# Two SwiGLU layers around a merged attention and retention: the odd 256 columns first, as plain products

## Chip, cores and metric

One core of one Trainium2 chip. The metric is device time of one execution in microseconds (us); the median of several runs is compared.

## What is computed

The input x has 512 rows of 1024 float32 values. One decoder layer is applied:

```
x = x + 1/2 * SwiGLU_1(RMSNorm(x))
h = RMSNorm(x); p = h @ w_in
a = NSA(p) @ w_branch_nsa ; r = Retention(p) @ w_branch_ret
x = x + (sigmoid(g_a) * a + sigmoid(g_r) * r) @ w_out
x = x + 1/2 * SwiGLU_2(RMSNorm(x))
out = RMSNorm(x) * final_norm

SwiGLU(x) = (silu(x @ w_gate) * (x @ w_up)) @ w_down     (1024 -> 2816 -> 1024)
RMSNorm(x) = x * rsqrt(mean(x*x) + 1e-6) * gain
```

NSA is an attention of 16 heads with three branches. Retention has 8 heads (key size 64, value size 128); its causal scores are multiplied by a decay, and each head's output is centred, divided by its own root mean square over 128 values and multiplied by a gain.

## The kernel before

Three stages follow each other: `ffn1`, `mix` (attention, retention and their output projections) and `ffn2`. All products are made from float32 values split into a rounded high part and a rest (`split`, L42): ScalarE (ACT) copies the high half at L45, VectorE (DVE) subtracts for the low half at L51, and TensorE (PE) adds three products in the fast 32-bit type f32r, high by high, high by low and low by high. Sums over partitions are products with a matrix of ones, in plain fp32.

**Gate and up** (`gate_up`, L369) go through the 2816 columns in blocks, five of 512 and one of 256 at the end. Each block is one `fast_block` (L261): x's transpose and the two weights are cut into halves of 256 rows and of 512 inner values, and seven Strassen products take the place of eight (order 1, 7, 2, 6, 5, 4, 3). A product has two units of 12 matmuls of 512 columns, 24 in all (in the last block one unit of 24 with 256 columns). The left operands A1 to A7 are made once per FFN from the four quarters of x (`scaled` L232 applies the gain on ACT, `combine` L236 forms s1, s2, s3 and s4, here named so, on DVE and splits all); the right operands are combined from loads on DVE (`put`, L278) and split for each product into the rings whi (3 buffers) and wlo (4). The gated results of a block are transposed by PE (`turn`, L380) behind product 1 of the next block.

**FFN 1's start** (L445 on): x is loaded in eight pieces, PE transposes each 128-column group over all 512 rows, ACT scales it, and `combine` runs after each half. The three norm gains come by three loads of single 4-byte elements (L1247).

**FFN 2's start**: the first half of the operands is made while w_out still runs, the second after its last product. `natural` transposes x back (L1175), 32 transposes in the first block.

**Down** (`down`, L406) needs eight PSUM accumulators, from a pool of its own that follows the pool of gate and up.

**Retention** (`ret_batch` L850, `ret_stage` L874, `ret_head` L896, `ret_norm` L933) runs with a background of gate and branch projections. `weave` (L145) issues the main generator under a raised priority of 400 and pulls background by credit. A head's scores are products at L909 and L910 into banks of a pool of three (name ra), which the transposes of q and k use too; its norm is one fp32 product over ones at L937, then a root on ACT, a reciprocal on DVE and a product on GpSimd.

The order on each engine is not that of the code: a scheduler places every instruction by its own model of the time and by the priorities.

Of the kernel before, what the change touches and what calls it, by code (L numbers as in the profile page):

```python
# [23 lines left out]
BLOCKS = (512,) * 5 + (256,)  # L24
FB = (6, 3, 3, 4)
# [11 lines left out]
class Layer:  # L37
# [158 lines left out]
    def rstd(self, pool, nat=False):  # L196
# [4 lines left out]
        nc.tensor.matmul(ps, self.ones, self.ss, start=True, stop=True)  # L201
# [10 lines left out]
    def lay(self, gu, tags):  # L212

        rings = dict(kept=FB[0], passing=FB[1], whi=FB[2], wlo=FB[3])
        for tag in tags:
            for _ in range(rings.get(tag, 2)):
                gu.tile([128, 4, 256], F32, name="lay", tag=tag, bufs=rings.get(tag, 2))

# [17 lines left out]
    def combine(self, q, act, A, X):  # L236
        nc = self.nc
        sub, add = ALU.subtract, ALU.add

        def hl(p, src):  # L240
            n = 4 // len(A[p][0])
            for i, (h, l) in enumerate(zip(*A[p])):
                self.split(h, l, src[:, i * n:i * n + n])

        if q == 0:
            hl(1, X[0][0])
            s3 = self.act_tile(act, "s3", [128, 4, 256])
            nc.vector.tensor_tensor(s3, X[0][0], X[0][1], op=sub)
            hl(7, s3)
            return  # L250
        hl(2, X[1][0])
        s1, s2 = [self.act_tile(act, n, [128, 4, 256]) for n in ("s1", "s2")]
        nc.vector.tensor_tensor(s1, X[0][1], X[1][1], op=add)
        nc.vector.tensor_tensor(s2, s1, X[0][0], op=sub)
        hl(6, s2)
        hl(5, s1)
        hl(4, X[1][1])
        nc.vector.tensor_tensor(X[1][0], X[1][0], s2, op=sub)
        hl(3, X[1][0])

    def fast_block(self, n, b, gu, psum, A, rn, between):  # L261

        nc = self.nc
        W = BLOCKS[b]
        f0 = sum(BLOCKS[:b])
        kk = 1024 // W
        nu = 4 // kk
# [33 lines left out]

        def product(ps, p, on=False):
            h, l = [[z[:, k] for z in pieces for k in range(z.shape[1])] for pieces in A[p]]
            for i in range(nu):
                src = need(p, i)
                hi = gu.tile([128, kk, W], F32R, name="whi", bufs=FB[2])
                lo = gu.tile([128, kk, W], F32R, name="wlo", bufs=FB[3])
                self.split(hi, lo, src)
# [11 lines left out]
            between.get(p, lambda: None)()  # L320
# [48 lines left out]
    def gate_up(self, n, gu, act, psum, A, rn, between):  # L369
# [4 lines left out]
        def turn(nat, W):  # L374
            for j in range(W // 128):
# [7 lines left out]
        for b, W in enumerate(BLOCKS):  # L383
            nat = self.fast_block(n, b, gu, psum, A, rn, between)
            between = {1: lambda nat=nat, W=W: turn(nat, W)}
        between[1]()
        return out

    def down_weights(self, n, dn, j, tail):

        W = []
        for k in (2 * j, 2 * j + 1):
            W.append([])
            for c in range(2):
                raw = (self.ring if j else dn).tile([128, 1, 512], F32, name="raw", bufs=4)
# [10 lines left out]
    def down(self, n, dn, psum, act, loads, tail, nat):  # L406


        acc = [psum.tile([128, S], F32, name="mm") for _ in range(8)]
# [13 lines left out]
        for j in range(NF // 2):  # L423
# [21 lines left out]
    def ffn1(self):  # L445
# [3 lines left out]
        with tp(name="gu", bufs=1, reuse_waits="tile") as gu, tp(name="ps1", bufs=2, space=PSUM, reuse_waits="tile") as psum:  # L449
            self.lay(gu, ("kept", "whi", "A3", "wlo", "A5", "A4", "A6", "A2", "A7", "A1", "passing"))  # L450
            xin = [gu.tile([128, D], F32, name="xin", tag=f"A{p}", bufs=2) for p in (5, 5, 3, 3)]
            for c in range(2):
                for t in range(NT):
                    cs = slice(c * 512, c * 512 + 512)
                    nc.sync.dma_start(out=xin[t][:, cs], in_=a["x"][0, t * 128:t * 128 + 128, cs])
            sums = self.small.tile([128, NT, 2], F32, name="sums", bufs=1)
            xT = [self.act_tile(act, "xT") for _ in range(4)]
            A, X = self.operands(gu, range(1, 8)), self.quarters(act)
            for k in range(ND):
                ps = psum.tile([128, S], F32, name="mm", tag=("pb", "pc", "tt")[k % 3], bufs=2)  # L460
                for t in range(NT):
                    nc.tensor.transpose(ps[:, t * 128:t * 128 + 128], xin[t][:, k * 128:k * 128 + 128], self.ident)
                self.scaled("ffn1_norm", k, ps, X)
                x = xT[k // 2][:, k % 2]
                nc.vector.tensor_copy(x, ps)
                nc.scalar.dma_start(out=self.xdram[k], in_=x)
                if k % 4 == 3:
                    self.combine(k // 4, act, A, X)
            rn = []

            def norm():
                for t in range(NT):
# [3 lines left out]
                ms = self.small.tile([128, NT], F32, name="ms4", bufs=1)  # L476
                nc.vector.tensor_tensor(ms, sums[:, :, 0], sums[:, :, 1], op=ALU.add)
                sd = self.small.tile([128, NT], F32, name="sd", bufs=2)
                nc.scalar.activation(sd, ms, AF.Sqrt, bias=self.eps, scale=1.0 / D)
                rn.append(self.small.tile([128, NT], F32, name="rn", bufs=2))  # L480
                nc.vector.reciprocal(rn[0], sd)

            norm()
            out = self.gate_up(1, gu, act, psum, A, lambda: rn[0], {})
        self.xt = tc.alloc_tile_pool(name="xt", bufs=1, reuse_waits="tile")
        self.xl_pool = tc.alloc_tile_pool(name="xl", bufs=1, reuse_waits="tile")
        self.xh, self.xl = [[z.tile([128, S], F32R, name=n, bufs=8) for _ in range(8)] for z, n in ((self.xt, "xh"), (self.xl_pool, "xl"))]
        self.mc = tc.alloc_tile_pool(name="mc", bufs=1, reuse_waits="tile")
        with tp(name="dn", bufs=1, reuse_waits="tile") as dn, tp(name="ps1d", bufs=8, space=PSUM, reuse_waits="tile") as psum:
# [12 lines left out]
            self.down(1, dn, psum, out, loads, tail, False)  # L502
            self.first = self.primed(self.dense_N(None, a["w_in"][0], C_KC, 512, ND, self.xh, self.xl))
        act.release()
# [369 lines left out]
    def ret_stage(self, h, T):  # L874
# [15 lines left out]
        if self.ret_tail:  # L890
            yield from self.ret_norm()
        if self.ret_next:
            yield from self.ret_head(*self.ret_next)
        self.ret_next = h, dec, T, vh, vl

    def ret_head(self, h, dec, T, vh, vl):  # L896
# [5 lines left out]
        for js in ((0,), (1, 3), (2,)):  # L902
# [16 lines left out]
            self.split(sh[:, 0:off], sl[:, 0:off], sd[:, 0:off], "act", "pool" if 1 in js else "dve")  # L919
            yield 1.8  # L920
            if pv:
# [8 lines left out]
        self.ret_tail = sq, r  # L930
        yield 1.0

    def ret_norm(self):  # L933
        nc = self.nc
        sq, r = self.ret_tail
        ps = self.psR.tile([128, S], F32, name="ra")
        nc.tensor.matmul(ps, self.ones, sq, start=True, stop=True)  # L937
# [42 lines left out]
    def mix(self):  # L980
# [11 lines left out]
        with tp(name="m", bufs=1, reuse_waits="tile") as self.m:  # L992
# [54 lines left out]
            with tp(name="psM4", bufs=4, space=PSUM, reuse_waits="tile") as pool, \  # L1047
# [22 lines left out]
                def retention():  # L1070
                    for b in range(4):
                        yield from self.ret_batch(b)
                    yield from self.ret_norm()
# [30 lines left out]
                self.xT = []  # L1104
                for k in range(ND):
# [7 lines left out]
                for c in range(2):  # L1113
# [11 lines left out]
        self.xl_pool.release()  # L1125
# [28 lines left out]
    def ffn2(self):  # L1154
# [3 lines left out]
        with tp(name="gu2", bufs=1, reuse_waits="tile") as gu, tp(name="ps2", bufs=2, space=PSUM, reuse_waits="tile") as psum:  # L1158
            self.lay(gu, ("kept", "passing", "A5", "A3", "A4", "A6", "whi", "A2", "wlo"))
            gu.tile([128, 4, 256], F32R, name="lay", tag="wlo", bufs=FB[3])  # L1160
            A, X = {**self.A2, **self.operands(gu, (5, 3, 4, 6, 2))}, self.X2
            for k in range(4, ND):
                self.scaled("ffn2_norm", k, self.xT[k], X)
            self.combine(1, act, A, X)
# [15 lines left out]
            out = self.gate_up(2, gu, act, psum, A, lambda: rn[0], {7: norm, 6: natural})  # L1180
        self.xt.release()
        with tp(name="dn2", bufs=1, reuse_waits="tile") as dn, tp(name="ps2d", bufs=8, space=PSUM, reuse_waits="tile") as psum:
            for n in ("ah", "al"):
                for _ in range(1 + TAIL // 2):
                    dn.tile([128, 2, 512], F32R, name=n, bufs=1 + TAIL // 2)
            for n in ("raw", "o"):
                for _ in range(4):
                    dn.tile([128, S], F32, name=n, bufs=4)
            fin = dn.tile([128, D], F32, name="fin", bufs=1)
            x = [dn.tile([128, D], F32, name="x", bufs=4) for _ in range(NT)]  # L1190
# [126 lines left out]
```

## Time and profile before

| | us |
|---|---|
| median of 3 runs (lowest, highest) | 1382.78 (1382.48, 1384.65) |
| the profiled execution | 1383.53 |
| its span | 1381.8 |
| PE busy | 1341.4 |
| DVE busy | 947.5 |
| ACT busy | 745.1 |
| PE idle, waiting for high halves (L45) in gate and up | 15.5 |

The profile describes one execution. Its page has the busy time of each engine over the span; the other views group waits, follow the chain of waits that ended last, cut the span into stretches, or list instructions in order of time. Start times are in us from the span's start. The duration of a matmul in a timeline overlaps with the next one's, so in a stream the distance of two starts is its price.

### The profile page before, as it was taken

What the parts mean: (1) busy time and instruction counts of PE and PEld (TensorE: products, weight loads), DVE (VectorE), ACT (ScalarE), POOL (GpSimd) and SP (SyncE); (2) the same over time, 40 slices, a digit from 0 to 9 for tenths busy, and PEclk for the clock granted to TensorE, in tenths of its full rate; (3) what the DMA queues carried; (4) which work ended last, traced back from release to release, by engine and by line L of the source; (5) the groups of instructions that cost most, each with busy time, mean ns of one, the idle gap of its engine ahead of it and who ended that gap; (6) DMA issues with size and microseconds to landing.
All of it is one profiled execution on the core that took longest, in us unless ns stands there. A gap on an engine that the chain in (4) does not pass through costs nothing.

```text
span 1381.8 us, 19828 instructions
## 1 busy us (share of the span) xinstructions
PE 1341.4 (97%) x7122; PEld 1143.5 (83%) x7122; DVE 947.5 (69%) x1594; ACT 745.1 (54%) x1348; POOL 318.6 (23%) x379
## 2 busy tenths in 40 slices
PE   6999999999999999999999999999979999999997
PEld 4788889788899889999997888887867888897886
DVE  6977887534545779877778788647667778874342
ACT  7555555434446656856774546444456565554243
POOL 0000000000211077768645335713220000000001
PEclk9999999999999999999999999999989999999999
DMA  8554441624425431112115334435436544424231
GB/s 289 183 167 147 145 137 63 204 92 140 153 73 156 122 89 43 47 47 85 47 49 176 126 101 132 133 132 197 146 114 221 168 142 149 136 92 160 99 122 62
DMA packets 120707, 175.73 MB, mean 127 GB/s; under 512 B 15904, under 2 KB 54432, under 8 KB 120608
## 3 DMA queue, kind: packets, MB, share of 16 engines
q1 hardware_dynamic: 106304, 151.77, 35.5%
q10 hardware_dynamic: 13024, 18.50, 3.7%
q0 software_dynamic: 1280, 4.20, 0.8%
q8 instruction: 56, 0.92, 0.3%
q14 instruction: 43, 0.35, 0.1%
HBM read 157.65 MB, written 16.78 MB: 126 GB/s over the span
## 4 chain that ended last, share of the span: by engine, by line
PE 88%; DVE 5%; DMA 3%; ACT 2%; issue 1%; POOL 1%; ACTq 0%; SPq 0%; DVEq 0%; POOLq 0%
PE mm L317 27%; PE mm L67 16%; PE mm L68 16%; PE mm L69 16%; PE t L777 2%; PE o L793 2%; PE o L792 2%; PE tt L380 1%; DVE wlo L51 1%; PE s L748 1%; PE s L749 1%; DMA ffn_norm<-in_ffn_norm_dram 1%; DMA b<-in_ffn_w_gate_dram 1%; ACT whi L45 1%; DMA b<-in_ffn_w_up_dram 1%
## 5 line engine op out<-in xcount | busy, mean ns | idle before, releaser
L317 PE MATMUL mm<-whi,Ah 128*128 128x512 f32 (+1 forms) x672 | 251.6, 380 | 15.8 <-ACT whi L45 15.5
L317 PE MATMUL mm<-whi,Al 128*128 128x512 f32 (+1 forms) x672 | 249.7, 377 | 0.0
L51 DVE TENSOR_TENSOR wlo<-raw,whi 128x512 fp32r<-128x512 f32 (+1 forms) x184 | 139.8, 770 | 145.8 <-ACT whi L45 143.2
L45 ACT ACTIVATE whi<-raw 128x512 fp32r<-128x512 f32 (+1 forms) x208 | 128.0, 623 | 206.4 <-PE mm L68 106.7
L45 ACT ACTIVATE whi<-b 128x1024 fp32r<-128x1024 f32 x154 | 161.2, 1060 | 119.9 <-PE mm L317 98.1
L51 DVE TENSOR_TENSOR wlo<-b,whi 128x1024 fp32r<-128x1024 f32 x154 | 187.5, 1227 | 46.2 <-ACT whi L45 45.8
L317 PE MATMUL mm<-wlo,Ah 128*128 128x512 f32 (+1 forms) x672 | 176.4, 376 | 2.5 <-DVE wlo L51 2.5
L317 PEld LDWEIGHTS mm<-whi,Ah 128*128 128x128 f32 x672 | 127.9, 191 | 41.0 <-ACT whi L45 18.8
L317 PEld LDWEIGHTS mm<-whi,Al 128*128 128x128 f32 x672 | 128.2, 191 | 21.6
L317 PEld LDWEIGHTS mm<-wlo,Ah 128*128 128x128 f32 x672 | 120.0, 190 | 27.2 <-DVE wlo L51 5.7
L278 DVE TENSOR_TENSOR b<-b,b 128x1024 f32<-128x1024 f32 x88 | 107.2, 1219 | 33.3 <-DMA b<-in_ffn_w_up_dram 33.0
L67 PE MATMUL mm<-whi,xh 128*128 128x256 f32 (+2 forms) x416 | 127.6, 308 | 0.0
L68 PE MATMUL mm<-wlo,xh 128*128 128x256 f32 (+2 forms) x416 | 126.9, 306 | 0.0
L69 PE MATMUL mm<-whi,xl 128*128 128x256 f32 (+2 forms) x416 | 126.6, 305 | 0.0
L754 ACT ACTIVATE P<-P,nm 128x128 f32<-128x128 f32 (+3 forms) x128 | 71.3, 559 | 34.0 <-DVE nm L753 33.3
L51 POOL TENSOR_TENSOR wlo<-raw,whi 128x512 fp32r<-128x512 f32 x56 | 73.7, 1317 | 66.1 <-ACT whi L45 64.7
L760 POOL TENSOR_SCALAR P<-P,rc,sgn 128x128 f32<-128x128 f32 (+3 forms) x128 | 76.9, 612 | 45.7 <-DVE rc L757 22.5
L68 PEld LDWEIGHTS mm<-wlo,xh 128*128 128x128 f32 x416 | 78.9, 190 | 3.4 <-issue 0.2
L67 PEld LDWEIGHTS mm<-whi,xh 128*128 128x128 f32 x416 | 78.7, 190 | 3.4 <-issue 0.2
L69 PEld LDWEIGHTS mm<-whi,xl 128*128 128x128 f32 x416 | 78.8, 190 | 3.1
L1223 POOL TENSOR_TENSOR x<-x,fin 128x512 f32<-128x512 f32 x4 | 5.1, 1286 | 324.2 <-ACT sq L1219 324.2
L67 PE MATMUL mm<-xh,whi 128*128 128x512 f32 x192 | 75.8, 395 | 0.0
(325 smaller groups left out, 3052.5 us busy)
## 6 DMA issues: line engine op xcount, KB each, us to landing
b<-in_ffn_w_up_dram SPq DMA_DIRECT2D x88, 512.0 KB, 4.4
raw<-in_w_in_dram SPq DMA_DIRECT2D x104, 256.0 KB, 2.8
b<-in_ffn_w_gate_dram SPq DMA_DIRECT2D x44, 512.0 KB, 3.8
raw<-in_ffn_w_down_dram SPq DMA_DIRECT2D x88, 256.0 KB, 2.7
rdram<-rsp ACTq DMA_DIRECT2D x16, 256.0 KB, 2.3
raw<-in_w_branch_nsa_dram SPq DMA_DIRECT2D x16, 256.0 KB, 2.7
raw<-in_w_branch_ret_dram SPq DMA_DIRECT2D x16, 256.0 KB, 2.7
raw<-in_w_out_dram SPq DMA_DIRECT2D x16, 256.0 KB, 2.9
```

The lines of the kernel that those rows point to most:

```text
L45: nc.scalar.activation(hi, src, AF.Copy)
L51: eng.tensor_tensor(lo, src, hi.bitcast(F32), op=ALU.subtract)
L67: mm(ps, ah, bh, start=start, stop=False)
L68: mm(ps, ah, bl, start=False, stop=False)
L69: mm(ps, al, bh, start=False, stop=stop)
L278: nc.vector.tensor_tensor(o, x, y, op=op)
L317: nc.tensor.matmul(ps[t][:, 0:W], y[K][:, t * 128:t * 128 + 128], (hi, lo)[w][:, k], start=not on and K == 0 and w == 0 and y is h, stop=l ...
L754: nc.scalar.activation(pb, pb, AF.Exp, scale=-1.0, bias=nm[:, br:br + 1], accum_out=sm[:, br:br + 1])
L760: nc.gpsimd.tensor_scalar(P[:, br, 0:w], P[:, br, 0:w], rc[:, br:br + 1], gate, op0=ALU.mult, op1=ALU.mult)
L777: nc.tensor.transpose(ps[:, n * w + j * 128:n * w + j * 128 + 128], P[:, br, j * 128:j * 128 + 128], self.ident)
L792: nc.tensor.matmul(o[:, q0:q1], v, PT[0][:, br, j, cs], start=half == 0 and br == 0 and j == 0, stop=False)
L793: nc.tensor.matmul(o[:, q0:q1], v, PT[1][:, br, j, cs], start=False, stop=False)
```

## The change

The 256 odd columns come first in each FFN, by 96 plain products of 512 columns (256 of gate beside 256 of up) in place of the seven Strassen products of 256 at the end. Five 512-column Strassen blocks follow, in the product order 1, 2, 7, 6, 5, 4, 3, with both loads of a product issued before its first split. In FFN 1, x is loaded, transposed and scaled by quarters, of 256 rows by 512 inner values, each ahead of the plain products that use it; s3, s1, s2, s4 and their splits are made inside the first Strassen block (`later`). In FFN 2 the weights of the plain block's first half are split while w_out runs. One PSUM pool with four tags holds the banks of gate and up and of down; down's products for its first two inner pieces come before the last transposes. The gains are loaded as rows and transposed by one PE instruction. Sums of squares for `rstd` and for the eight heads are split and made by two f32r products. A head's norm is issued behind the first scores of the next head, and the first head's scores are issued without raised priority. The core of the diff:

```diff
-BLOCKS = (512,) * 5 + (256,)
+W0, NB = 256, 5
...
-            if ahead:
+            if ahead and self.lead:
                 with self.tc.high_priority(offset=ahead):
...
-        nc.tensor.matmul(ps, self.ones, self.ss, start=True, stop=True)
+        sh, sl = [self.tmp.tile([128, S], F32R, name=n, tag="sq", bufs=2) for n in ("ssh", "ssl")]
+        self.split(sh, sl, self.ss)
+        nc.tensor.matmul(ps, self.onesR, sh, start=True, stop=False)
+        nc.tensor.matmul(ps, self.onesR, sl, start=False, stop=True)
...
+    def later(self, act, A, X):
...
+        def s3():
+            self.both(A[7], combined("s3", X[0][0], X[0][1], ALU.subtract))
+        def s2():
+            combined("s1", X[0][1], X[1][1], ALU.add)
+            self.both(A[6], combined("s2", new["s1"], X[0][0], ALU.subtract))
+        def s4():
+            self.nc.vector.tensor_tensor(X[1][0], X[1][0], new["s2"], op=ALU.subtract)
+            self.both(A[3], X[1][0])
+        return {(1, 0): s3, (2, 0): s2, (7, 0): lambda: self.both(A[5], new["s1"]), (6, 0): s4}
...
+    def plain_block(self, n, psum, Q, units, rn, hooks):
...
+        acc = [psum.tile([128, 512], F32, name="mm", tag=tag, bufs=2) for tag in ("pb", "pb", "pc", "pc")]
+        for q in range(2):
+            W = None
+            for u in range(2):
+                hooks.get((q, u), lambda: None)()
+                W = W or units(q)
+                h, l = self.by_k(Q[u][q])
+                for i, (hi, lo) in enumerate(W):
+                    for w in range(2):
+                        for k in range(2):
+                            for y in ((h, l), (h,))[w]:
+                                for t in range(2):
+                                    nc.tensor.matmul(acc[2 * u + t], y[2 * i + k][:, t * 128:t * 128 + 128], (hi, lo)[w][:, k],
+                                                     start=q == i == w == k == 0 and y is h, stop=q == i == w == k == 1)
...
+            srcs = [need(p, i) for i in range(nu)]
...
+                if i == 0:
+                    hook(p, 0)
...
+        Y = banks("p" + ty)
+        product(Y, 2)
+        lower = gated(s1, Y, 0)
         Z = banks("p" + tz)
         product(Z, 7)
         sZ = snap(Z)
-        Y = banks("p" + ty)
-        product(Y, 2)
-        lower = gated(s1, Y, 0)
         product(X, 6, True)
...
+            if j == 0:
+                for i in range(8):
+                    if i == 3:
+                        turn((0, 1))
+                    if i == 6:
+                        turn((2, 3))
+                        acc += [psum.tile([128, S], F32, name="mm", tag="tt", bufs=2) for _ in range(2)]
+                    for k in (0, 1):
+                        mm(i, k, a, W)
+                continue
...
+            out, turn = self.gate_up(1, gu, act, psum, A, Q, units, lambda: rn, {
+                (0, 0): lambda: quarter(0, 0), (0, 1): lambda: quarter(1, 0), (1, 0): lambda: quarter(0, 1), (1, 1): rest},
+                self.later(act, A, X))
...
-        if self.ret_tail:
-            yield from self.ret_norm()
         if self.ret_next:
+            if h == 1:
+                yield 2.0
+                self.lead = False
+                yield 0.0
             yield from self.ret_head(*self.ret_next)
...
+            self.lead = True
             yield 1.8
+            if self.ret_tail and 0 in js:
+                yield from self.ret_norm()
...
-        nc.tensor.matmul(ps, self.ones, sq, start=True, stop=True)
+        nc.tensor.matmul(ps, self.onesR, sh, start=True, stop=False)
+        nc.tensor.matmul(ps, self.onesR, sl, start=False, stop=True)
...
-                        self.combine(0, act, self.A2, self.X2)
+                        self.both(self.A2[1], self.X2[0][0])
+                        self.both(self.A21, self.X2[0][1])
+                        self.w2 = tc.alloc_tile_pool(name="w2", bufs=1, side="right", reuse_waits="tile")
+                        self.early = []
...
-            nc.scalar.dma_start(out=g, in_=a[n][0].rearrange("(k p) -> p k", p=128))
+            nc.scalar.dma_start(out=self.graw[i * ND:i * ND + ND, :], in_=a[n][0].rearrange("(k p) -> k p", p=128))
```

**FFN 1's start on ACT.** The operands of the left side are Ah (high) and their DVE partner Al; xg are scaled quarters, whi weights. Before, after the squares of x:

```order
L45 ACTIVATE Ah_154<-s3_198 128x1024 [waits DVE_49]
L45 ACTIVATE whi_297<-b11_295 128x1024 [waits DMAHW4_49]
L466 DMA xdram_69<-xT_140 128x512 [waits DMAHW0_49,DVE_49]
L45 ACTIVATE Ah_144<-xg_158 128x1024 [waits Activation_49]
L45 ACTIVATE Ah_148<-xg_159 128x1024 [waits Activation_49]
L45 ACTIVATE whi_324<-b12_319 128x1024 [waits DVE_49]
```

and now, in rows 41 to 50 of the engine:

```order
L573 ACTIVATE sd_140<-ms4_391,both_80 128x2 [waits DVE_49]
L45 ACTIVATE Ah_150<-xg_164 128x1024 [waits Activation_49]
L556 ACTIVATE xg_165<-tt_349,gain_84 128x256 [waits PE_49]
L556 ACTIVATE xg_165<-tt_349,gain_84 128x256
L556 ACTIVATE xg_165<-tt_359,gain_84 128x256 [waits PE_49]
L556 ACTIVATE xg_165<-tt_359,gain_84 128x256
L45 ACTIVATE whi_321<-b0_186 128x1024 [waits DMAHW1_49,PE_49]
L45 ACTIVATE Ah_160<-s3_453 128x1024 [waits DVE_49]
L45 ACTIVATE Ah_154<-xg_165 128x1024 [waits Activation_49]
L45 ACTIVATE whi_437<-b11_433 128x1024 [waits PE_49]
```

The last quarter's operand (now Ah_154) stands behind the squares and the scaling of all four quarters, and behind the first Strassen combination (Ah_160, of s3).

**The first head's scores on PE** (rT are the transposed q and k of that head; Oh and whi, xh belong to the background). Before:

```order
L910 MATMUL ra<-rT_8353,rT_8355 128x384
L909 MATMUL ra<-rT_8353,rT_8354 128x128
L910 MATMUL ra<-rT_8353,rT_8355 128x128
L67 MATMUL mm<-whi,xh 128x512
...
L909 MATMUL ra<-rT_8353,rT_8354 128x256 [waits DVE_49,PE_49]
L910 MATMUL ra<-rT_8353,rT_8355 128x256
L67 MATMUL mm<-Oh,whi 128x512 [waits PE_49,Activation_49]
```

and now (L1043 and L1044 are the lines L909 and L910 of before):

```order
L1043 MATMUL ra<-rT_8271,rT_8272 128x128
L1044 MATMUL ra<-rT_8271,rT_8273 128x128
L1044 MATMUL ra<-rT_8271,rT_8273 128x512
L67 MATMUL mm<-whi,xh 128x512
...
L1043 MATMUL ra<-rT_8271,rT_8272 128x256 [waits DVE_49,PE_49]
L1044 MATMUL ra<-rT_8271,rT_8273 128x256
L67 MATMUL mm<-Oh,whi 128x512 [waits PE_49,Activation_49]
```

The earlier score products stand elsewhere among the background's; the third pair, which waits for a bank, stands behind nine background products in both, and ahead of the same one.

**FFN 2's first Strassen block on DVE**, between products 7 and 6 on PE. wlo are low halves of weights (11384 for product 5, unit 0), xg the quarters, Al the low halves of A5 (10955), A6 (10961) and A3 (10957). Before, the sums s1 and s2 stood directly behind the last additions to x, ahead of the first block:

```order
L1117 TENSOR_TENSOR xT_10572<-xT_10572,mm_10777 128x512 [waits DMASW7_49,PE_49]
L253 TENSOR_TENSOR s1_10992<-xg_10576,xg_10578 128x1024 [waits Activation_49]
L254 TENSOR_TENSOR s2_10993<-s1_10992,xg_10575 128x1024 [waits DVE_49]
L51 TENSOR_TENSOR wlo_11010<-b11_11007,whi_11009 128x1024 [waits DMAHW7_49,Activation_49]
L51 TENSOR_TENSOR Al_10981<-xg_10577,Ah_10980 128x1024 [waits Activation_49]
```

and now:

```order
L51 TENSOR_TENSOR wlo_11384<-b12_11377,whi_11383 128x1024 [waits Activation_49]
L260 TENSOR_TENSOR s1_11258<-xg_10536,xg_10538 128x1024
L335 TENSOR_TENSOR g_11280<-snap_11232,mm_11236 128x512 [waits PE_49]
L335 TENSOR_TENSOR g_11281<-snap_11233,mm_11237 128x512 [waits PE_49]
L260 TENSOR_TENSOR s2_11260<-s1_11258,xg_10535 128x1024 [waits DVE_49]
L51 TENSOR_TENSOR Al_10955<-s1_11258,Ah_10954 128x1024 [waits Activation_49]
L271 TENSOR_TENSOR xg_10537<-xg_10537,s2_11260 128x1024 [waits DVE_49]
L51 TENSOR_TENSOR Al_10961<-s2_11260,Ah_10960 128x1024 [waits Activation_49]
L51 TENSOR_TENSOR Al_10957<-xg_10537,Ah_10956 128x1024 [waits Activation_49]
```

The combinations moved from ahead of the first block into it, behind a low half of product 5.

## Rows read from the trace of the kernel before

**Rows 1.** Page, busy time of each engine over the span
```profile
PE 1341.4 (97%) x7122; PEld 1143.5 (83%) x7122; DVE 947.5 (69%) x1594; ACT 745.1 (54%) x1348; POOL 318.6 (23%) x379
```

**Rows 2.** PE's waits: what was waited for, us in total, times, longest
```profile
PE mm L317 <- ACT whi L45: 15.5, 8, 5.1
PE mm L462 <- DMA xin<-in_x_dram: 4.8, 3, 3.8
PE ra L909 <- DVE rT L869: 3.2, 1, 3.2
PE mm L67 <- ACT thi L45: 2.7, 2, 1.4
```

**Rows 3.** The chain of waits: start, duration, what
```profile
1.86 8.36 DMA ffn_norm<-in_ffn_norm_dram
...
33.63 1.14 DVE xg L258
...
48.25 22.06 PE mm L317 x96
...
76.91 0.87 PE tt L380 x8
...
234.75 12.36 PE mm L317 x103
...
751.45 0.70 DVE rT L869
...
940.98 0.64 ACT rh L45
```

**Rows 4.** Stretches: us, busy (instructions) by engine, PE clock, DMA share, GB/s
```profile
0.00:48.25 48.25, 33.86 (x128) 24.18 (x129) 37.23 (x41) 35.57 (x61) 0.70 (x6) 0.93 0.68 229
1011.77:1050.60 38.83, 30.41 (x138) 24.60 (x137) 34.00 (x32) 30.17 (x44) 10.39 (x12) 0.87 0.42 134
72.10:112.25 40.15, 40.15 (x186) 33.08 (x185) 31.25 (x32) 22.33 (x29) 0.00 (x0) 1.00 0.52 157
10.60:14.00 3.40, 1.06 (x10) 0.82 (x8) 2.33 (x3) 3.40 (x11) 0.00 (x0) 1.00 1.05 395
14.00:20.80 6.80, 5.32 (x12) 3.81 (x12) 5.89 (x8) 6.80 (x16) 0.00 (x0) 0.50 1.05 407
20.80:35.00 14.20, 11.63 (x45) 7.89 (x44) 14.20 (x15) 12.06 (x17) 0.00 (x0) 1.00 0.65 246
758.00:800.00 42.00, 42.00 (x194) 34.13 (x193) 32.02 (x44) 20.03 (x34) 13.19 (x15) 1.00 0.40 127
1014.00:1020.90 6.90, 3.87 (x11) 3.10 (x11) 5.84 (x4) 6.90 (x11) 3.92 (x3) 0.51 0.00 0
```

**Rows 5.** Groups of ACT from 0 to 48.25: count, busy us, mean ns, idle
```profile
L45 ACT ACTIVATE whi<-b 128x1024 fp32r<-128x1024 f32 x10 | 10.6, 1094 | 5.0 <-DVE b L278 4.2 <-DVE wlo L51 0.8
L234 ACT ACTIVATE xg<-mm,ffn_norm 128x256 f32<-128x256 f32 x16 | 6.4, 514 | 2.4 <-PE mm L462 2.4
L475 ACT ACTIVATE sq<-xin 128x512 f32<-128x512 f32 x8 | 5.3, 681 | 0.0
...
L475 ACT ACT_TABLE_LOAD x1 | 1.3, 1283 | 3.6 <-issue 3.6
```

**Rows 6.** Groups of DVE from 0 to 48.25, columns as above
```profile
L278 DVE TENSOR_TENSOR g<-snap,mm 128x512 f32<-128x512 f32 x2 | 1.4, 680 | 0.0
```

**Rows 7.** Timeline of PE around the first head's scores: start, duration, what
```profile
752.29 0.55 PE L909 MATMUL ra<-rT,rT 128*128 128x256 f32 x1 [3.16 <-DVE rT L869]
...
752.86 0.63 PE L67 MATMUL mm<-Oh,whi 128*128 128x512 f32 x1
753.28 0.63 PE L68 MATMUL mm<-Ol,whi 128*128 128x512 f32 x1
```

**Rows 8.** Timeline of PE at the first head sum
```profile
771.56 1.02 PE L937 MATMUL ra<-sq,ones 128*128 128x512 f32 x2
...
772.64 0.39 PE L910 MATMUL ra<-rT,rT 128*128 128x512 f32 x1
```

More of the change, by code (lines that the diff above doesn't have):

```diff
@@ L217, in lay, with lay_banks @@
                 gu.tile([128, 4, 256], F32, name="lay", tag=tag, bufs=rings.get(tag, 2))
+    def lay_banks(self, psum, tags):
+        for tag in tags:
+            for _ in range(2):
+                psum.tile([128, S], F32, name="lay", tag=tag, bufs=2)
     def operands(self, gu, ps):
@@ L261, in fast_block, with both, a21, combined @@
-    def fast_block(self, n, b, gu, psum, A, rn, between):
+    def both(self, hl, src):
+        n = 4 // len(hl[0])
+        for i, (h, l) in enumerate(zip(*hl)):
+            self.split(h, l, src[:, n * i:n * i + n])
+    def a21(self, act):
+        return [[act.tile([128, 4, 256], F32R, name="a21", tag="act", bufs=11)] for _ in range(2)]
+    def later(self, act, A, X):
+        new = {}
+        def combined(name, x, y, op):
+            new[name] = self.act_tile(act, name, [128, 4, 256])
+            self.nc.vector.tensor_tensor(new[name], x, y, op=op)
+            return new[name]
+        def s3():
[7 more added lines that the diff above has]
+        return {(1, 0): s3, (2, 0): s2, (7, 0): lambda: self.both(A[5], new["s1"]), (6, 0): s4}
@@ L367, in fast_block, with gate_up, turn @@
         return lower + upper
-    def gate_up(self, n, gu, act, psum, A, rn, between):
+    def gate_up(self, n, gu, act, psum, A, Q, units, rn, first, hooks):
         nc = self.nc
         out = []
-        def turn(nat, W):
-            for j in range(W // 128):
+        def turn(nat, js):
+            for j in js:
                 if j % 2 == 0:
@@ L381, in turn @@
                 nc.scalar.activation(out[-1][:, j % 2], ps, AF.Copy)
[L383 to L387, printed above, removed]
+        nat = self.plain_block(n, psum, Q, units, rn, first)
+        hooks = {**hooks, (1, "e"): lambda nat=nat: turn(nat, range(W0 // 128))}
+        for b in range(NB):
+            nat = self.fast_block(n, b, gu, psum, A, rn, hooks)
+            hooks = {(1, "e"): lambda nat=nat: turn(nat, range(4))}
+        return out, lambda js: turn(nat, js)
     def down_weights(self, n, dn, j, tail):
@@ L404, in down_weights, with down @@
         return W
-    def down(self, n, dn, psum, act, loads, tail, nat):
-        acc = [psum.tile([128, S], F32, name="mm") for _ in range(8)]
+    def down(self, n, dn, psum, act, turn, loads, tail, nat):
+        acc = [psum.tile([128, S], F32, name="mm", tag=tag, bufs=2) for tag in ("pb", "pb", "pa", "pa", "pc", "pc")]
         held = []
@@ L451, in ffn1 @@
             xin = [gu.tile([128, D], F32, name="xin", tag=f"A{p}", bufs=2) for p in (5, 5, 3, 3)]
[L452 to L455, printed above, removed]
             sums = self.small.tile([128, NT, 2], F32, name="sums", bufs=1)
+            sd = self.small.tile([128, NT], F32, name="sd", bufs=2)
+            rn = self.small.tile([128, NT], F32, name="rn", bufs=2)
@@ L457, in ffn1 @@
+            a21 = self.a21(act)
             xT = [self.act_tile(act, "xT") for _ in range(4)]
             A, X = self.operands(gu, range(1, 8)), self.quarters(act)
[L459 to L468, printed above, removed]
@@ L473, in norm @@
+            def norm(u):
+                ts = slice(2 * u, 2 * u + 2)
+                for t in (2 * u, 2 * u + 1):
                     for c in range(2):
@@ new lines, in units @@
+            def units(q):
+                W = []
+                for i in range(2):
+                    hi, lo = self.rings(1, gu)
+                    src = raws[2 * q + i]
+                    if q:
+                        self.split(hi, lo, src)
+                    else:
+                        for k in range(2):
+                            self.split(hi[:, k], lo[:, k], src[:, k])
+                    W.append((hi, lo))
+                return W
+            load(0, 0)
+            ps = psum.tile([128, S], F32, name="tt", bufs=2)
```

221 lines of the change are left out of this document (149 added, 72 removed).

## The prediction, made before the changed kernel ran

> **What bounds the kernel now.** I read the busy line of the page first: TensorE (PE) is busy for 97% of the span [rows 1]. So a change pays only if it takes work from PE or fills one of its few pauses; work moved between the other engines counts only where PE comes to wait for it. The profiled execution took 1383.53 us with a span of 1381.8; the median of the three runs is 1382.78. I make the sum against the execution and take 0.75 off at the end. A measurement here tells about 0.2%, 2.8 us, from no change.
>
> Second, PE's waits by releaser [rows 2]: 15.5 us for high halves that ScalarE (ACT) writes, 4.8 for x, 3.2 for a retention tile, 2.7 for the first down-projection halves. Third, the chain of waits, for where they lie and for PE's prices [rows 3]: 96 products of 512 columns in 22.06 us, 0.230 each; 103 of 256 columns in 12.36, 0.120 each; 8 transposes in 0.87, 0.109 each. Fourth, stretches [rows 4]: a middle block (72.1 to 112.25) leaves PE no pause, with VectorE (DVE) at 31 of 40 us, while in the first 48.25 us of FFN 1 and in the 38.8 us after w_out PE is short of operands. The granted clock shows a second loss there: 0.50 or 0.51, that is 1.2 instead of 2.4 GHz, in short stretches behind a pause.
>
> **FFN 1.** Up to 48.25 PE has run 96 products and 32 transposes [rows 4], worth 96 x 0.230 + 32 x 0.109 = 25.6 us: 22.6 are lost. What remains of gate and up then is 744 products of 512 and 168 of 256, 171.1 + 20.2 = 191.3 us. After the change the first 96 products are the plain block's, and 5 x 168 of 512 remain, 193.2 us: the plain block costs PE 1.9 more than the Strassen block it replaces. That is sure; the start must earn it.
>
> When does the plain block end? ACT leads. In its new order stand, from the first scaling to the last operand (Ah_154), 20 pieces of 256 columns at 0.40 (6.4 us for 16), 4 splits of 512 at 0.64, 7 squares at 0.66, 6 splits of 1024 at 1.06 and a table load of 1.28 [rows 3, 5], and about 2 us of roots and DMA issues: 24.8 us. The scalings wait for the gains. Today the third gain load lands at 10.2 [rows 3]; by rows it is the same 4 KB in 8 pieces, and the trace has no such load. Bounds are 3.8, PE's longest wait for x now [rows 2], and 10.2; with one transpose and a copy behind the load I take 6.5. Then Ah_154 is there at 31.3, its low half 1.2 later, and 24 products (5.5) remain: 38, and with 8 products of the next block that stand between them about 39 (36 to 42 by the bounds). Gain 48.25 - 39 = 9.2, less 1.9.
>
> New cost: s3, s1, s2 and s4 are now made inside block 0, on DVE. From the end of product 2 to the low half of A6, which product 6 needs, DVE has six 1024-wide operations at 1.14 from start to start [rows 3] and two 512-wide at about 0.65 (0.68 busy [rows 6]): 8.1 us, against product 7's 24 x 0.230 = 5.5. PE waits 2.6. FFN 1 gains **4.7** (0 to 10).
>
> **The down projections.** Products for j = 0 now come before the last transposes of g, but by the order 12 transposes still stand first and thi is still split behind the copies of av on ACT. Of the 2.7 us waited for thi and some half clock behind it I take **2.0** for both (0 to 4).
>
> **Head sums and rstd.** From 771.56 to 772.64 PE does one fp32 product over ones and one f32r product [rows 8]: 1.08 - 0.23 = 0.85. Two f32r products cost 0.46. So 0.39 x 9 = **3.5** us. Each adds a split, 0.64 on ACT and about 0.7 on DVE, beside a PE that is full while DVE has 32 of 42 us and ACT 20 [rows 4]; it is hidden, and if it were not, the next head's scores would cover it, since the norm now stands behind them. The last norm stands ahead of background products that are left, so the wait behind it at 940.98 [rows 3] goes: **0.3**.
>
> **First head without priority: 0.** The wait to remove is 3.16 us before the third score product at 752.29 [rows 7]. It ends with DVE's rT of the second head at 751.45 [rows 3], which frees the bank of the k transposes. After the change the first two score products come elsewhere among the background, but the waiting third comes behind the same number of background products, and DVE, ACT, GpSimd and the queues are in the same order up to it. What released it is unmoved, so I keep the wait and the half clock behind it.
>
> **FFN 2.** From 1011.77 to 1050.6 PE ran 96 products, 32 transposes and 8 tiny sums (0.5): 26.1 of 38.8 us, 12.7 lost. After the change the plain block's first 48 products (11 us) have operands that were split during w_out, and ACT's 8 scalings, split and norm fit into them. I allow 1 us: the block ends at 1011.8 + 22.1 + 0.5 + 1 = 1035.4. Then 193.2 us of products and 3.5 of transposes follow, and one new wait. In DVE's order the low half of product 5's first unit (wlo_11384) stands before s1, g, s2 and A6; its buffer is that of product 7's last unit, so it starts when product 7 has ended. From there ACT needs 1.06, DVE six operations of 1.14 and two of 0.65: 9.2 us, with 2.2 of transposes and first products on PE meanwhile. PE waits 7.0, and a pause of 5.1 at 1011.5 was followed by 6.9 us at 0.51 [rows 4], of which PE used 3.9, half of it lost: 0 to 1.9, I take 1.2. Before: 1050.6 + 191.3 = 1241.9. After: 1035.4 + 193.2 + 3.5 + 7.0 + 1.2 = 1240.3. Gain **1.6** (-1 to 10).
>
> **Sum:** 4.7 + 2.0 + 3.5 + 0.3 + 0 + 1.6 = 12.1. 1383.5 - 12.1 - 0.75 gives **1370.6 us**. Loads don't bound any of it: at 14.0 to 20.8 they run at 407 GB/s, from then to 35 us at 246 [rows 4], before the plain block has used its weights.
>
> **Rivals.**
> (a) The first head works as named: without priority its bank comes free before PE reaches the third product. For it: the two leading products do move. Against: the releaser does not. It gives back 3.2 and the half clock, 12 products at 0.43 instead of 0.23 [rows 7], 2.4: 1365.0. Chance 0.10.
> (b) No wait at product 6 in either FFN: a DVE that gets ahead during the plain block finishes the combinations early. For it: a middle block leaves DVE 9 of 40 us [rows 4]. Against: the order puts operations behind a buffer that product 7 holds, and an engine does not pass its own queue. Back come 2.6 + 7.0 + 1.2 = 10.8: 1359.8. Chance 0.18.
> (c) Slower than before: the plain block is fed through ACT in short bursts, and PE's clock stays at 1.2 GHz over it. At 14.0 to 20.8 PE ran 5.3 of 6.8 us, and the clock was 0.50, behind a stretch in which it had run 1.1 of 3.4. One plain block at that clock costs 96 x (0.43 - 0.23) = 19.2 more: 1389.8. From 61 products at 1.2 GHz on the change loses. Against it: from 20.8 to 35 PE was busy for 11.6 of 14.2 us, in pieces, and the clock was 1.00 throughout. Chance 0.09. The Trainium skill, "TensorE: Matmul & The Clock Gate", section "A second HAM failure mode: psum-queue depth-cycling", speaks against this change in the same sense: where PE idles briefly but often between groups of matmuls, the clock goes back and forth between its two levels. By that rule the plain block of FFN 1, fed in four quarters, would run at the lower level for much of its length, and this rival's time would follow; the stretch from 20.8 to 35 does not bear it out, the one from 14.0 does.
> (d) The change does not do what it says: x by quarters is only as fast as the gains, x and ACT allow, and the waits inside block 0 eat both starts. FFN 1 and FFN 2 then give 0 instead of 6.3: 1377, and up to 1382 if product 6 waits longer. Chance 0.13.
>
> **Numbers.** The forecast has 0.50. The range holds it, (a), (b) and most of (d): 1355 to 1381; left out are (c) and the ends. Faster by over 0.2% (below 1380.0): 0.50 + 0.10 + 0.18 + 0.09 of (d) = 0.87. Within 0.2%: 0.05. Slower: 0.08, nearly all of (c).
>
> **What would show it.** Right: PE's plain block ends near 39 us, the next waits are at product 6 of block 0 in both FFNs (about 2.6 and 7 us, for the halves of A6), fp32 products over ones are gone and the pairs take 0.46, PE's wait before the third score product of the first head is still 3 us, followed by 0.50 in the clock; a middle block is still 40.2 us. Wrong: a plain block ending after 44, a granted clock of 0.50 over more than 10 us of it, pauses of PE in the retention where DVE must now split the head sums, or a wait for weights in the first 48 us.

## The result, and the profile after

The median of four runs is 1374.53 us (1372.68 to 1377.48), against 1382.63 before: a ratio of 0.9942, with an interval of 0.9930 to 0.9954. The change is faster by 8.1 us, forecast 12.1; the time lies in the range. The profiled execution took 1372.68 us with a span of 1370.9, so the stage by stage account below, span against span, has 10.9 us to explain; this execution is the fastest of the four.

PE's waits in the kernel after, in the columns of [rows 2]:

```profile
PE tt L549 <- DMA xin<-in_x_dram: 4.8, 2, 3.8
PE mm L376 <- ACT Ah L45: 3.8, 1, 3.8
PE ra L1043 <- DVE rT L1001: 3.3, 1, 3.3
PE mm L376 <- DVE Al L51: 2.4, 2, 1.4
PE mm L309 <- ACT a L45: 1.8, 1, 1.8
PE tt L655 <- DVE rsd L1049: 1.4, 1, 1.4
```

The 15.5 us for high halves of the weights (L45) are gone. In their place stand the halves of the left operands: Ah and Al, 3.8 and 2.4 us, both at product 6 (Al 1.4 in FFN 1 and 1.0 in FFN 2). The wait of the first retention head is the size it was. One is new: transposes of k wait 1.4 us for rsd, the multiplication that empties a bank of scores.

Where the span went, by the first and last products of each stage (start times in the two timelines): to the first product of the first down projection, 249.91 before and 242.38 after, 7.5 us are won; from there to the end of w_out, 761.9 against 760.5, 1.4; from there to the first product of the second down projection, 240.3 against 240.5, 0.1 lost; from there to the end, 129.7 against 127.5, 2.1. That is 10.9.

Stretches of the kernel after, in the columns of [rows 4]:

```profile
0.00:39.73 39.73, 31.86 (x137) 25.39 (x138) 26.51 (x41) 29.34 (x57) 0.70 (x6) 1.00 0.84 292
39.73:62.40 22.67, 21.32 (x97) 17.03 (x95) 21.00 (x21) 15.34 (x21) 0.00 (x0) 1.00 0.31 92
1003.05:1026.09 23.04, 23.04 (x105) 18.76 (x104) 16.85 (x18) 15.33 (x24) 5.83 (x4) 1.00 0.45 139
1047.00:1056.00 9.00, 3.95 (x14) 2.64 (x15) 8.57 (x9) 5.94 (x9) 1.07 (x2) 0.70 0.52 173
1055.00:1057.50 2.50, 2.50 (x8) 1.97 (x7) 0.57 (x1) 0.07 (x1) 0.00 (x0) 0.53 0.04 7
746.80:750.00 3.20, 3.20 (x10) 2.45 (x9) 2.40 (x7) 3.07 (x7) 1.59 (x2) 0.50 0.82 291
```

The plain block of FFN 1 ends at 39.7 us; that of FFN 2 takes 23.0 us without a pause. The row of FFN 1's block has a granted clock of 1.00 from 0 us on, but its first products do not run at that pace. In the timeline of PE:

```profile
11.53 1.20 PE L309 MATMUL mm<-whi,Ah 128*128 128x512 f32 x2
12.53 0.80 PE L309 MATMUL mm<-whi,Al 128*128 128x512 f32 x2
...
14.07 0.61 PE L309 MATMUL mm<-whi,Ah 128*128 128x512 f32 x2
14.53 0.62 PE L309 MATMUL mm<-whi,Al 128*128 128x512 f32 x2
```

Two products take 1.0 us from start to start at 11.53 and 0.46 at 14.07. The first seven of the block, from 7.67 to 12.5 us, start 0.40 to 0.59 apart, about half pace; from 13 us on a product takes 0.227.

From 1047 to 1056 PE works 3.95 of 9 us, with DVE busy for 8.57, and behind it the clock is near 0.5.

What no row of the prediction covers shows in the chain of waits (start, duration, what). In the kernel before, the two FFNs ran at one pace, 15.22 us for 67 products or 0.2272 each, first line in FFN 1 and second in FFN 2:

```profile
117.92 15.22 PE mm L317 x67
...
1120.07 15.22 PE mm L317 x67
```

In the kernel after they do not. The same piece of code, a middle Strassen block, in FFN 1 (first two lines) and in FFN 2 (the others):

```profile
168.01 5.49 PE mm L376 x24
...
174.38 31.56 PE mm L376 x139
...
1086.12 5.57 PE mm L376 x24
...
1092.56 32.27 PE mm L376 x139
...
1126.86 5.57 PE mm L376 x24
...
1133.30 32.27 PE mm L376 x139
```

139 products take 31.56 us in FFN 1 and 32.27 in FFN 2, 0.2270 and 0.2322 each, at the same granted clock and with no pause in either. A block takes 207.98 - 168.01 = 39.97 us there and 1126.86 - 1086.12 = 40.74 here.

### The profile page after: what moved, and what is told of

Read it like the earlier page. It is cut to its first block, busy times and chain, and to the rows that moved or that the text cites. A ratio compares the mean times of both kernels' runs of the same rounds, so it can differ in the third digit from the quotient of the medians.

```text
span 1370.9 us, 19559 instructions
## 1 busy us (share of the span) xinstructions
PE 1338.7 (98%) x6979; PEld 1135.4 (83%) x6979; DVE 930.4 (68%) x1591; ACT 738.0 (54%) x1347; POOL 320.0 (23%) x379
## 4 chain that ended last, share of the span: by engine, by line
PE 88%; DVE 5%; DMA 3%; ACT 1%; issue 1%; POOL 1%; SPq 0%; ACTq 0%; DVEq 0%; POOLq 0%
PE mm L376 26%; PE mm L67 16%; PE mm L69 16%; PE mm L68 16%; PE mm L309 3%; PE t L909 2%; PE o L925 2%; PE o L924 1%; PE tt L442 1%; DVE wlo L51 1%; PE s L880 1%; PE s L881 1%; DMA rq<-rdram 1%; DMA b<-in_ffn_w_up_dram 1%; DMA xin<-in_x_dram 1%
## 5 line engine op out<-in xcount | busy, mean ns | idle before, releaser
L45 ACT ACTIVATE whi<-raw 128x512 fp32r<-128x512 f32 (+1 forms) x212 | 131.0, 624 | 215.0 <-PE mm L68 115.8
L51 DVE TENSOR_TENSOR wlo<-raw,whi 128x512 fp32r<-128x512 f32 (+1 forms) x188 | 135.8, 730 | 145.6 <-ACT whi L45 138.5
L376 PE MATMUL mm<-whi,Ah 128*128 128x512 f32 x560 | 220.6, 395 | 4.0 <-ACT Ah L45 3.8
L376 PE MATMUL mm<-whi,Al 128*128 128x512 f32 x560 | 221.1, 395 | 2.4 <-DVE Al L51 2.4
L45 ACT ACTIVATE whi<-b 128x1024 fp32r<-128x1024 f32 (+1 forms) x148 | 153.2, 1047 | 121.7 <-PE mm L376 89.7
L51 DVE TENSOR_TENSOR wlo<-b,whi 128x1024 fp32r<-128x1024 f32 (+1 forms) x148 | 175.8, 1210 | 49.8 <-ACT whi L45 49.4
L376 PE MATMUL mm<-wlo,Ah 128*128 128x512 f32 x560 | 161.0, 394 | 0.3 <-DVE wlo L51 0.3
L376 PEld LDWEIGHTS mm<-whi,Ah 128*128 128x128 f32 x560 | 105.5, 189 | 28.2 <-ACT Ah L45 4.0
L376 PEld LDWEIGHTS mm<-whi,Al 128*128 128x128 f32 x560 | 105.6, 189 | 26.4 <-DVE Al L51 3.5
L376 PEld LDWEIGHTS mm<-wlo,Ah 128*128 128x128 f32 x560 | 104.2, 188 | 22.4 <-DVE wlo L51 0.5
L335 DVE TENSOR_TENSOR b<-b,b 128x1024 f32<-128x1024 f32 x80 | 96.5, 1224 | 33.4 <-DMA b<-in_ffn_w_up_dram 32.7
```

The lines of the kernel that those rows point to most:

```text
L45: nc.scalar.activation(hi, src, AF.Copy)
L51: eng.tensor_tensor(lo, src, hi.bitcast(F32), op=ALU.subtract)
L335: nc.vector.tensor_tensor(o, x, y, op=op)
L376: nc.tensor.matmul(ps[t][:, 0:W], y[K][:, t * 128:t * 128 + 128], (hi, lo)[w][:, k], start=not on and K == 0 and w == 0 and y is h, stop=l ...
```

## Experiments

**Where the two paces come from.** Two things were compared: the distance of successive starts of 512-column products, from the traces, and the addresses that the compiled program gives their two operands within a partition. Mean distance in us (and number of products) by the difference of the two start addresses, modulo 256 bytes, where the products before and behind have 512 columns too and no pause lies between:

| kernel | difference 0 | another difference |
|---|---|---|
| before | 0.2275 (2916) | 32: 0.2333 (907) |
| after | 0.2279 (2556) | 32: 0.2329 (1513) |

The change moves 32 bytes. By the addresses of the two programs it is a tile of FFN 1's start, ms4 (means of squares), that does it: it has two buffers in place of one, and each small tile fills a slot of 32 bytes. (The gains, three tiles of 32 bytes before and one of 96 now, take the same room.) The left-hand pools behind it moved up by 32, the right-hand ones, at the end of memory, did not. FFN 2's high halves now lie in a right-hand pool (w2) while the left operands lie in left-hand ones. The place alone does not matter: FFN 1's operands both begin at 160 modulo 256 before and both at 192 now, and run at 0.227 either way. In the kernel before, the epsilon tile made the same 32 bytes of difference for 960 products, from the first down projection to w_out.

Both offsets made equal (the second pad is FFN 2's):

```diff
-        self.gneps = self.mc.tile([128, 1], F32, name="gneps", bufs=1)
...
+        pad = tc.alloc_tile_pool(name="pad", bufs=1, side="right")
+        pad.tile([128, 8], F32, name="pad")
         act = tc.alloc_tile_pool(name="act", bufs=1, side="right", reuse_waits="tile")
...
+                self.pad = tc.alloc_tile_pool(name="pad2", bufs=1, side="right")
+                self.pad.tile([128, 8], F32, name="pad")
                 self.act = act = tc.alloc_tile_pool(name="act2", bufs=1, side="right", reuse_waits="tile")
...
+        self.gneps = both[:, 3:4]
```

> The changed kernel with two moves in memory and no instruction more or less on PE: the tile of the group norm's epsilon lies in a free column of another constant, so that everything in the attention stage lies 32 bytes lower, and a 32-byte pad lies above the right-hand pools. By the program's addresses both operands of every product of 512 columns then begin at the same offset within 64 bytes; in the changed kernel 1616 of 4458 differ by 32. Address theory: a product whose two operands differ by 32 takes 0.2327 us in a stream, one whose operands agree 0.2267 (the two paces in the traces of before and of the change); here all run at 0.2267, 1616 x 0.0056 = 9.0 us less than the changed kernel: about 1365.5. Rival: the pace belongs to the stage (which engines write and which loads run beside it), so FFN 2 stays at 0.232 and the time at 1374.

1363.51 us (ratio to before 0.9863, 0.9849 to 0.9878): 11.0 less than the change. The chain of this kernel in FFN 2:

```profile
1080.01 5.50 PE mm L376 x24
...
1086.37 31.55 PE mm L376 x139
```

0.2270, FFN 1's pace. The pace does not belong to the stage. The count gave 9.0; the spans of the two profiled executions, 1370.9 and 1361.9, differ by just that, the medians by 11.0. The count left something out: in FFN 2 of the changed kernel the low halves, whose addresses agree, ran at 0.231 on average between the others, 0.004 more than alone. For some 310 products that is 1.2, and 10.3 in all.

The pad alone:

> The changed kernel with the 32-byte pad above the right-hand pools alone. The high halves of the weights of FFN 2 then agree with the left operands; 976 products of the attention stage and of the first down projection still differ. Address theory: FFN 2 goes from 0.232 to 0.227, the attention stage stays: 640 x 0.0056 = 3.6 us by count, up to 4.6 if the aligned low halves between them were slowed too: 1370 to 1371. Rival (the pace belongs to the stage): no change, 1374.

1370.09 us (0.9912, 0.9894 to 0.9931), 4.4 less than the change: FFN 2's share. The kernel before, with the epsilon tile moved alone:

> The kernel before with the epsilon tile moved in the same way: its products whose operands differ by 32 go from 969 to 9 (middle of the first down projection, gates, both output projections). Address theory: 960 x 0.0056 = 5.4 us less than before: 1377.3; the change itself would then be worth about 12 us between the two aligned kernels. Rival: 1382.6.

1377.98 us (0.9964, 0.9951 to 0.9976), 4.6 less than before. So between the two aligned kernels the change is worth 1377.98 - 1363.51 = 14.5 us, and 6.4 of these (11.0 - 4.6) were lost to addresses.

How far must they agree? Pads of 96 and of 160 bytes (24 and 40 in place of 8 in the diff above) leave everything else as it is:

> The kernel of the aligned experiment with a pad of 96 bytes in place of 32: the high halves of the weights of FFN 2 and the left operands then begin at the same offset within 64 bytes, but 64 bytes apart within 128. If 64 bytes is the unit that counts, FFN 2 runs at 0.227 and the time is the aligned kernel's, 1363.5. If it is 128, FFN 2 is back at 0.232: 1367 to 1368.

> The aligned kernel with a pad of 160 bytes: high halves of the weights of FFN 2 and the left operands agree within 128 bytes, and are 128 apart within 256. If 128 bytes is the unit that counts, FFN 2 runs at 0.227 and the time is 1363.5; if it is 256 or more, 0.232 and 1367 to 1369.

1368.78 us (0.9896, 0.9880 to 0.9913) and 1368.02 (0.9896, 0.9881 to 0.9912). The chains in FFN 2, of 96 bytes first:

```profile
1082.20 5.57 PE mm L376 x24
```

```profile
1081.55 5.58 PE mm L376 x24
```

Both are slow again: 64 apart, 606 products at 0.2326; 128 apart, 603 at 0.2321. 256 apart is fast: in the aligned kernel 1543 products differ by 256 within 512, at 0.227. The expectation of 64 fell, and 128 with it; the unit is 256 bytes as far as these differences tell.

**FFN 2's product 6.** s1, s2 and A6 issued ahead of the transposes of x, and with them s3 and A7, which stood behind (by their programs, this run and the next ones, but for "both together", keep the address differences of the changed kernel):

```diff
-            s3 = hooks[1, 0]
+            s3, s2 = hooks[1, 0], hooks.pop((2, 0))
...
+                s3()
+                s2()
                 natural()
-                s3()
```

> The changed kernel with one move in FFN 2: s1, s2 and the halves of A6 are issued ahead of the transposes of x, so that on DVE they stand before the first Strassen block's weights. Prediction's theory (the wait at product 6 is the place in DVE's queue behind a half whose buffer product 7 holds): PE's waits of 3.8 and 1.0 us for A6 go, and with them the 0.50 clock behind: 5 to 6 us, 1368.5 to 1369.5. Rival (DVE and ACT are simply out of time in that block): the wait turns up earlier, in the second half of the plain block or at product 7, and the time stays within 2 us of 1374.

1366.57 us (0.9882, 0.9867 to 0.9896), 8.0 less than the change, where 5 to 6 were expected. The trace lists no wait of PE between 990 and 1060 us at all. In the changed kernel it had these:

```profile
1047.25 1.14 PE L442 MATMUL tt<-ident,g 128*128 128x128 f32 x8 [0.85 <-ACT xn L1344]
1052.19 1.22 PE L376 MATMUL mm<-whi,Ah 128*128 128x512 f32 x2 [3.80 <-ACT Ah L45]
1054.41 0.79 PE L376 MATMUL mm<-whi,Al 128*128 128x512 f32 x1 [1.00 <-DVE Al L51]
...
1057.14 1.19 PE L376 MATMUL mm<-wlo,Ah 128*128 128x512 f32 x4
```

The waits are 5.6 us. The six products from 1054.41 to 1057.14 took 2.73 us, 1.3 more than at 0.232, and the two before them lost another 0.6 at the same clock: 7.5 of the 8.0. DVE had the time; its queue had the wrong order.

**Both together:**

> The changed kernel with both: operands that begin at the same offset within 64 bytes everywhere, and s1, s2 and A6 issued early in FFN 2. If the two gains lie on different things (pace of the products, a wait in one block) they add up: 1374.5 - 11.0 - 8.0 = 1355.5. If the faster pace in FFN 2 only makes PE wait longer for operands, part of it is lost: 1358 to 1362.

1355.26 us (0.9803, 0.9788 to 0.9819): the two add up, and this version beats both kernels, by 26.8 and 19.3 us. From the end of w_out to the second down projection, where neither version has a wait at product 6, the trace of s2 first takes 232.3 us and this one 227.8: 4.5, FFN 2's share of the addresses once more. Its PE waits:

```profile
PE tt L551 <- DMA xin<-in_x_dram: 4.0, 2, 3.5
PE ra L1046 <- DVE rT L1004: 3.3, 2, 3.1
PE tt L658 <- DVE rsd L1052: 1.8, 1, 1.8
PE mm L309 <- ACT a L45: 1.4, 1, 1.4
PE mm L376 <- DVE Al L51: 1.4, 1, 1.4
```

**The first head's priority**, given back (the line that clears the flag is left out):

> The changed kernel, with the first head's scores under raised priority as before (the flag is never cleared). Prediction's theory: the wait before the third score product is ended by the second head's rT on DVE either way, so 3.2 to 3.5 us of wait stay and the time is within 1 us of the changed kernel's 1374.5. Rival: the part gave something (a shorter stretch at 0.50 behind the wait), and the time is 1 to 3 us longer.

1374.90 us, the changed kernel's time. The wait in its timeline of PE:

```profile
746.28 0.36 PE L1042 MATMUL ra<-rT,rT 128*128 128x256 f32 x1 [3.47 <-DVE rT L1001]
```

This flag does nothing here, as forecast.

**The head sums.** One fp32 product in place of the pairs, in rstd too, the norm left behind the scores:

```diff
...
-        self.split(sh, sl, sq)
-        self.ret_tail = sh, sl, r
+        self.ret_tail = sq, r
...
-        nc.tensor.matmul(ps, self.onesR, sh, start=True, stop=False)
-        nc.tensor.matmul(ps, self.onesR, sl, start=False, stop=True)
+        nc.tensor.matmul(ps, self.onesF, sq, start=True, stop=True)
```

> The changed kernel with the sums over ones in rstd and in the eight heads as one fp32 product again, without the splits; the norm stays behind the next head's scores. Prediction's theory: 0.36 to 0.39 x 9 = 3.2 to 3.5 us longer than the changed kernel, 1377.9. Rival: the two splits per head load ACT and DVE and hold banks, so that half of it is given back, and without them the time is only 1 to 2 us longer, 1376.

1378.51 us (0.9972, 0.9959 to 0.9984), 4.0 longer than the change, near the forecast. The pairs kept, the norm ahead of the next head's scores again:

```diff
-            if self.ret_tail and 0 in js:
-                yield from self.ret_norm()
...
+        if self.ret_tail:
+            yield from self.ret_norm()
         if self.ret_next:
...
+                    yield from self.ret_norm()
                     yield from self.ret_head(*self.ret_next)
```

> The changed kernel with a head's norm issued ahead of the next head's scores again, with the two f32r products. Theory from the trace after (the norm's bank, held behind the first scores, makes the transposes of k wait 1.4 us at 834 for the score banks): that wait goes, and the wait of the last head's chain, 0.3 to 1 us, comes back: 1373.5 to 1375. Rival, the prediction's (the norm behind the scores hides the split and the root): PE waits at each head's sum, 1 to 4 us longer, 1376 to 1378.

1382.99 us (0.9995, 0.9983 to 1.0008), 8.5 longer; both expectations were wrong. PE's waits of this kernel from 741 to 1010 us:

```profile
PE mm L67 <- ACT rh L45: 6.2, 1, 6.2
PE ra L1045 <- DVE rT L1001: 3.4, 1, 3.4
PE ra L1077 <- ACT rsh L45: 1.9, 2, 1.4
PE ra L1078 <- DVE rsl L51: 1.5, 2, 1.3
```

The 1.4 us for the score bank did go, but PE now waits 3.4 (1.9 + 1.5) for the splits of the sums and 6.2 for the last head's result, with a granted clock of 0.50 from 934.6 to 944.6, during that wait and behind it. Both undone:

> The changed kernel with both parts of the head norm as before: one fp32 product, issued ahead of the next head's scores. With pairs alone ahead the time was 1383.0 (last head's chain waited for, 6.2 us, and 3.4 us for the splits), with fp32 alone behind it was 1378.5. If the two parts work independently: 1374.5 + 8.5 + 4.0 = 1387. If the split is what makes the early place dear (the fp32 product needs no split, and the kernel before had a wait of 0.3 us there): 1378 to 1380, and the place of the norm by itself is worth little.

1377.12 us (0.9961, 0.9946 to 0.9976), 2.6 longer than the change, with an interval that overlaps the change's. So the parts are not independent: apart they cost 8.5 and 4.0, both undone not 12.5 but 2.6. Two f32r products need the later place; without them the place is worth nothing that the runs show (1378.51 and 1377.12). In the traces the stage from the first down product to the end of w_out takes 760.5 us with both, 764.0 with fp32 behind, 771.1 with the pairs ahead and 764.2 with fp32 ahead.

**The norm vectors** by single elements again:

> The changed kernel with the three norm vectors loaded by single elements as before, into the columns of the gain tile; no transpose of them and no copy. Prediction's theory: the third load lands near 10.2 as in the kernel before instead of ACT starting its first scaling at 6.2, and everything ACT does ahead of the plain block moves by up to 4 us; PE's wait at the first product grows, and since ACT leads until the last quarter is scaled, 2 to 4 us reach the end: 1376.5 to 1378.5. Rival (x's quarters arrive so late that the gains are covered, the second quarter's x comes at 11 us anyway): within 1 us of 1374.5.

1375.95 us (0.9937, 0.9916 to 0.9957); the interval overlaps that of the change, so a gain is not shown. The reason I had given did fail: in its timeline ACT's first scaling starts early.

```profile
5.74 0.84 ACT L552 ACTIVATE Ah<-tt,gain 128x256 fp32r<-128x256 f32 x2 [0.21 <-PE tt L549]
```

5.74 us, earlier than the 6.22 of the change. FFN 1 needs the first of the three loads alone, and that one is soon there. (In the kernel before, too, the first scaling began at 8.07, ahead of the third load's landing at 10.2.) All the same FFN 1 may lose something. In this trace PE has a wait at the start that none of the eleven other traces of the changed kernel and its variants has:

```profile
PE tt L549 <- DVE xT L558: 2.5, 2, 1.6
```

Its first down product starts at 244.97, in the eleven others between 241.3 and 243.5. Why DVE's copies come late here was not followed.

## Why the prediction was right, and where not

- **The total** is nearer than its terms. In the two traces FFN 1 gave 1.8 more than forecast, the stage between the FFNs 2.4 less, FFN 2's gate and up 1.7 less and its down projection 1.1 more; that these nearly cancel is luck. By the medians the change gave 8.1 of 12.1.
- **FFN 1** (4.7, and half of 2.0 for its down projection): 7.5. The plain block ended at 39.7, forecast 39 (the forecast's own terms, 38 and eight products, make 39.8), and the wait at product 6 was 1.35 us, forecast 2.6. The middle blocks too became shorter, 39.97 instead of the 40.15 of [rows 4]. The term that was too large is the wait; I had let DVE's chain begin at the end of product 2 with nothing done ahead, and in the trace s1 and s2 start at 46.6 and 47.9, before that end at 49.7.
- **The gains' landing** was a wrong step with a right number: I took the third load (10.2 in [rows 3]) for what the first scaling waits for. It needs the first.
- **Head sums and rstd** (3.5, and 0.3 for the tail): the whole stage from the first down product to the end of w_out gave 1.4. PE's work did shrink, a fp32 product costs 0.86 and a pair 0.50 (0.23 and 0.27 from start to start) instead of the 0.46 I took; nine times 0.36 is 3.2, and without the pairs the time was 4.0 longer. What the step left out is a new wait, 1.4 us of the transposes of k for a bank of scores (rsd, in the waits above). That it comes from the norm's sum holding one of the three banks behind the first scores is likely but not shown: it goes when the norm stands ahead, but with one fp32 product behind the scores it is not there either. Another 0.5 us is only order: four transposes of g now stand behind the first down products. I also wrote that the split is hidden, and that otherwise the next head's scores would cover it. Only the second half holds: the experiment without that cover took 8.5 us longer.
- **First head, 0:** right. 3.3 us stay, with rT as the releaser, with or without the priority.
- **FFN 2** (1.6, and half of 2.0): 0.1 lost up to the down projection, 2.1 won behind it. The plain block took 23.0 us (forecast 23.6), the pauses at product 6 were 0.8, 3.8 and 1.0, 5.6 in all (forecast 7.0), with the clock at 0.53 behind. These steps held. The step that failed is the price of what follows: 840 products at 0.230 on both sides of the sum, where the trace has 0.2272 before and 0.2322 after. That is 840 x 0.0050 = 4.2 us, and the pad alone, which gives 0.227 back, is worth 4.4. Both FFNs of the kernel before ran at the same pace, so the sum had no hint of it there; but from the first down projection to w_out 907 products already ran at 0.2333, which the prediction did not look at.
- **Rivals.** (b), no wait at product 6, was the right reading of what is possible (DVE had the time) but the order decided, as forecast; 8.0 us came back when it was mended. (c) did not happen: the half pace of FFN 1's first seven products ends by 13 us, and then a product takes 0.227 through pauses of 1.8 and 0.5 us; FFN 2's plain block ran at 1.00 throughout. The Trainium skill's rule on brief pauses between groups of matmuls ("TensorE: Matmul & The Clock Gate", "A second HAM failure mode: psum-queue depth-cycling") is not borne out there; from 13 us on the trace shows 0.50 only at the pauses of 3.3 and 5.6 us and at the kernel's end. (d) happened in FFN 2 alone, and for another reason.

## What to carry to other kernels

When code is moved or a small tile gets a second buffer, look where the operands of TensorE's products come to lie: pools that slide by 32 bytes against others cost 6.4 of the 14.5 us that the change earns here, and no wait and no clock shows it. Read the price of a product from the start-to-start distance in each stage, not once for the kernel. And before an operation is split into cheaper ones, ask what hides the added steps: the same two products were worth +4.0 us in one place of the order and -5.9 in the other (1382.99 against 1377.12).

## What the runs showed of the hardware

Streams of f32r products of 512 columns ran at 0.227 us each where the two operands' start addresses within the partition agreed modulo 256 bytes, and at 0.232 to 0.233 where they were 32, 64 or 128 apart, at the same granted clock and without pauses: 2 to 3% of a product's time. Products with equal addresses between unequal ones were slowed too, to 0.230 to 0.231 on average. That it is the reading of the two operands that collides is a guess; other differences, and products of fewer columns, were not tried.
